# One weight split behind the first sums of x, one bank copy ahead of a cast, in the first pair of gate and up

## The chip, the core and the metric

The kernel runs on one core of a Trainium2 chip. The core's engines work side by side, each through its own list of instructions in order: TensorE (PE) multiplies matrices into eight banks of PSUM, VectorE (DVE) and ScalarE (ACT) do elementwise work, GpSimd (POOL) does a little of it, and SyncE (SP) issues the transfers from memory. They wait for each other through semaphores. The metric is the time of one execution on the device, in microseconds (us); smaller is better. The engine names of the profile are used below; L506 is line 506 of the kernel.

## What is computed

A decoder trunk of two layers over 512 positions of width 1024. Each layer is a mixer (convolution and attention in layer 0, linear and latent attention in layer 1), a layer norm, a dense SwiGLU feed-forward net of width 2816, and a layer norm. The change lies in the feed-forward net, which comes once in each layer:

```python
def swiglu(x, w_gate, w_up, w_down):
    return (jax.nn.silu(x @ w_gate) * (x @ w_up)) @ w_down

x = layer_norm(ALPHA * x + y, ln_mix_g[layer], ln_mix_b[layer])
x = layer_norm(ALPHA * x + swiglu(x, ffn_w_gate[layer], ffn_w_up[layer], ffn_w_down[layer]),
               ln_ffn_g[layer], ln_ffn_b[layer])
```

All inputs and outputs are float32.

## The kernel before

**Numbers in two parts.** Every float32 operand of a matrix product is split into a rounded high part and the rest: a cast on ACT writes the high part, a subtraction on DVE the low part (`split`, lines 97 to 104). A product is then three matmuls: high by high, high by low, low by high.

**Gate and up** (`ffn`, from line 379). x is held transposed in `xh` and `xl` (high and low part), eight tiles of 128 features by 512 positions. Its four blocks of 128 positions come out of the layer norm one after the other; `flip` transposes a block on PE (L275), casts it into `xh` on ACT (L279), subtracts into `xl` on DVE (L280), and then copies it to a float32 tile `m` on ACT (L284). The first two tiles of 128 gate and up columns are computed directly, as four weights with one bank each. `lower` multiplies the first 256 positions, and takes the last two blocks through their flips in between; `upper(0)` and `upper(1)` multiply the other 256 positions, for the first and the second of these tiles; `finish` takes the silu on ACT (L393) and multiplies on DVE (L394).

**The pairs.** The other 20 tiles are done in pairs, each by seven products in place of eight, after Winograd's form of Strassen's method (`sevens`, from line 443). It works on sums of quarters of the weights and sums of quarters of x:

- `sums(sx)` makes the sums of x once in each layer. `s1` is the first of them: two differences on DVE (L355), and their split into tiles `hx` (cast on ACT, subtraction on DVE). `s2_sum` and `s2` (L361, L366, L367), `s3` and `s4` (L372 and splits) follow.
- `total(i)` makes the sum of weights that product i needs, if it needs one: on DVE (L483), into the tiles `lng` and `lnb`, or by an accumulating transfer that POOL issues (L474, for i = 4).
- `make(i)` issues the fetches that are due (`fetch_for`, L459, on SP), calls `total` for i + 1, and splits weight i. For i = 5 the call of `total(6)` comes after the split.
- `take(i)` runs product i on PE (L506, 24 matmuls of 256 columns; the first pairs open a bank with one matmul of 512 columns, the prime of L521) and moves the result on. In this method a bank is passed on: `take(0)` copies its bank to a second one (L533), `take(1)` copies its bank to a tile (L537), `take(2)` copies its bank to a third one (L541) to which the product of `take(4)` then adds, and `take(4)` copies that to a fourth (L549) to which `take(6)` adds.

Weights are split up to four products ahead (AHEAD = 4). There are five buffers for fetched weights and five for split ones.

**The order** is written out by hand: inside `tc.manual_schedule` (line 398) the instructions of each engine run in the order in which the program makes them. So a call that is moved in `ffn` moves its instructions in the queues of PE, ACT, DVE, POOL and SP alike, and an instruction that waits holds up all that stand behind it on its engine. `down`, which multiplies by the third weight, follows the pairs, and the kernel goes through `mixer0`, `ffn`, `mixer1`, `ffn`.

Of the kernel before, what the change touches and what calls it, by code (L numbers as in the profile page):

```python
# [34 lines left out]
AHEAD = 4  # L35
# [10 lines left out]
def trunk(ctx, tc, a, out):  # L46
# [21 lines left out]
    def nm(s):  # L68
        cnt[0] += 1
        return f"{s}{cnt[0]}"  # L70

    def slot(dt=F32):
        return wk.tile([P, 512], dt, tag="wk", name=nm("wk"))
# [305 lines left out]
    def ffn(layer, last, flips):  # L379
        hs = []  # L380
        m8 = {}

        def hidden_tile(f):
            if f < WK:
                return slot()
            if not m8:
                m8["t"] = big.tile([P, 8, S], F32, tag="m8", name=nm("m8"))
            return m8["t"][:, f - WK, :]

        def finish(f, pg, pu):  # L390
            h = hidden_tile(f)
            t = temp()
            act(out=t, in_=pg, func=AF.Silu)  # L393
            tt(out=h, in0=t, in1=pu, op=ALU.mult)  # L394
            hs.append(h)

        E = mybir.EngineType
        with tc.manual_schedule(engines={E.PE, E.Activation, E.DVE, E.Pool, E.SP}):
            first, sx = [], {}

            def lower(flip):
                w, bank = first[-1]
                gemm_a(bank, w, cols=slice(0, 256), ks=range(4))
                if flip:
                    flips.pop(0)()
                gemm_a(bank, w, cols=slice(0, 256), ks=range(4, KD))

            def upper(f):
                for w, bank in first[2 * f:2 * f + 2]:
                    gemm_a(bank, w, cols=slice(256, 512))  # L410

            ready = state["ready"]
            for i in range(4):
                first.append((ready.pop(0), ps()))
                if i < 2:
                    ready.append(weight())
                if i == 3:
                    make, take, n = sevens(sx, hs, hidden_tile)
                    make(0)
                lower(i % 2)  # L420
            s1, s2_sum, s2, s3, s4 = sums(sx)
            s1()
            upper(0)
            finish(0, first[0][1], first[1][1])
            s2_sum()
            upper(1)
            make(1)
            make(2)
            finish(1, first[2][1], first[3][1])
            s2()  # L430
            make(3)
            take(0)
            s3()
            make(4)
            s4()
            for i in range(AHEAD + 1, n + AHEAD):
                if i < n:
                    make(i)
                take(i - AHEAD)
        gb = load_ln("ffn", layer)  # L440
        return down(hs, [1] * (KF - 5) + [5], gb, last)

    def sevens(sx, hs, hidden_tile):

        pairs = list(range(DIRECT, KF, 2))
        n = 7 * len(pairs)
        base = state["i"]  # L450
        state["i"] += 4 * len(pairs)
        state["sums"] = 0
        raw, ws, tiles = {}, {}, {}

        def fetch_quarter(p, name, which):

            raw[p, name] = rawp.tile([P, D], F32, tag="raw", name=nm("raw"))
            i = base + 4 * p + which
            nc.sync.dma_start(out=raw[p, name], in_=a["w"][i // 2, :, (i % 2) * D:(i % 2) * D + D])  # L459


        loads = {}
        for p in range(len(pairs)):
            for at, args in ((-5, ("x", 0)), (-4, ("u", 1)), (-2, ("y", 2)), (-1, ("z", 3))):
                loads.setdefault(7 * p + at, []).append((p, *args))

        def total(i):

            if i >= n:
                return  # L470
            p, pos = divmod(i, 7)
            if pos == 4 and p == 0:
                q = base + 2
                nc.gpsimd.dma_start(out=raw[p, 4], in_=a["w"][q // 2, :, (q % 2) * D:(q % 2) * D + D],  # L474
                                    accum_op=ALU.add)
            elif pos == 4:
                tt(out=raw[p, 4], in0=raw[p, "u"], in1=raw[p, "y"], op=ALU.add)
            elif pos in (1, 2, 6):
                tag = ("lng", "lnb")[state["sums"] % 2]
                state["sums"] += 1  # L480
                raw[p, pos] = big.tile([P, D], F32, tag=tag, name=nm(tag))
                r, s = {1: ("x", "u"), 2: (1, "y"), 6: (2, "z")}[pos]
                tt(out=raw[p, pos], in0=raw[p, r], in1=raw[p, s], op=ALU.add)  # L483

        def make(i):

            fetch_for(i)
            p, pos = divmod(i, 7)
            raw[p, 4] = raw[p, "u"]
            if i != 5:  # L490
                total(i + 1)
            hi, lo = pair()
            split(raw[p, ("x", 1, 2, "z", 4, "y", 6)[pos]], hi, lo)
            if i == 5:
                total(i + 1)
            ws[i] = [t.rearrange("p (f k m) -> p f k m", f=2, k=4) for t in (hi, lo)]

        def quarter(k0, t0):
            return [[t[:, k0 + 2 * j:k0 + 2 * j + 2, t0:t0 + 256] for j in range(2)] for t in (xh, xl)]

        def product(bank, w, x, start=True):
            hi, lo = w
            for f in range(2):
                for k in range(4):
                    for m, (l, r) in enumerate(((hi, x[0]), (hi, x[1]), (lo, x[0]))):
                        mm(bank[:, f * 256:f * 256 + 256], lhsT=l[:, f, k, :], rhs=r[k // 2][:, k % 2, :],  # L506
                           start=(start and f == 0 and k == 0 and m == 0), stop=(k == 3 and m == 2),
                           skip_group_check=True)

        def take(i):  # L510


            p, pos = divmod(i, 7)
            g = tiles
            w = ws.pop(i)

            def primed():

                bank = ps()
                if p == 0 or (p == 1 and pos == 0):  # L520
                    mm(bank, lhsT=w[0][:, 0, 0, :], rhs=xh[:, 0, :], start=True, stop=True)  # L521
                return bank

            def half(n, gate, up):
                for f in range(2):
                    c = slice(f * 256, f * 256 + 256)
                    stt(out=g["h"][f][:, n * 256:n * 256 + 256], in0=gate[:, c], scalar=-1.0, in1=up[:, c],
                        op0=ALU.mult, op1=ALU.mult)

            if pos == 0:  # L530
                g["a"], g["d"] = ps(), primed()
                product(g["a"], w, quarter(0, 0))
                nc.scalar.copy(out=g["d"], in_=g["a"])  # L533
            elif pos == 1:
                g["b"], g["p5"] = ps(), temp("p")
                product(g["b"], w, sx["s1"])
                nc.scalar.copy(out=g["p5"], in_=g["b"])  # L537
            elif pos == 2:
                g["e"] = primed()
                product(g["d"], w, sx["s2"], start=False)  # L540
                nc.scalar.copy(out=g["e"], in_=g["d"])  # L541
            elif pos == 3:
                product(g["a"], w, quarter(4, 0), start=False)
                g["g0"] = temp()
                act(out=g["g0"], in_=g["a"], func=AF.Silu)
            elif pos == 4:
                product(g["e"], w, sx["s3"], start=False)
                g["f"], g["up1"] = primed(), temp("p")
                nc.scalar.copy(out=g["f"], in_=g["e"])  # L549
                tt(out=g["up1"], in0=g["p5"], in1=g["e"], op=ALU.add)  # L550
            elif pos == 5:
                product(g["d"], w, sx["s4"], start=False)
                up0 = temp("p")
                tt(out=up0, in0=g["p5"], in1=g["d"], op=ALU.add)
                g["h"] = [hidden_tile(pairs[p] + f) for f in range(2)]
                half(0, g["g0"], up0)
            else:
                product(g["f"], w, quarter(4, 256), start=False)
                g1 = temp()
                act(out=g1, in_=g["f"], func=AF.Silu)  # L560
                half(1, g1, g["up1"])
                hs.extend(g["h"])

        def fetch_for(i):
            for args in loads.get(i, ()):
                fetch_quarter(*args)

        for at in range(-5, 0):
            fetch_for(at)
        return make, take, n  # L570


    def mixer0():
# [658 lines left out]
```

## Time and profile before

| | |
|---|---|
| runs without a profile | 1083.64, 1085.29, 1083.64 us; median 1083.64 |
| the profiled execution, its own time | 1085.82 us |
| its span, from the first to the last instruction | 1083.9 us |
| mean granted clock of TensorE in it | 0.994 of full speed |
| gate and up, layer 0: from the first lower half to the last product | about 173 to 406 us |
| gate and up, layer 1 | about 724 to 956 us |

The profile is one execution, recorded by the chip; times in it count from the first instruction. Its views are: busy time by engine; who waited for whom; the instructions of one engine in order of time (the timeline: start, duration, engine, line, operation, output and inputs, count; in brackets the idle time before it and who ended that); and stretches of time (windows), with the busy time of each engine and then the granted clock, the share of the transfer engines, and GB/s. In the timeline neighbours of one kind are merged; the duration of a merged row reaches from the first start to the last end, and the matmuls in it follow each other faster than one of them lasts, since they are pipelined. How far apart they start is read from the starts of two rows and the count between them.

### The profile page before, as it was taken

The page shows a single profiled execution, that of the slowest core. Times are in us where ns is not written, and L with a number is a line of the kernel's source. Part 1 is how long each engine was busy: PE and PEld are TensorE (multiplying, and loading weights), DVE is VectorE, ACT ScalarE, POOL GpSimd, SP SyncE. Part 2 cuts the span into 40 slices and gives each one's busy share as a digit, 9 for nine tenths or more (in the row PEclk, how much of TensorE's full clock was granted, in tenths as well). Part 3 has the DMA queues.
Part 4 walks back from the last instruction along what each step waited for, and adds up shares of the span by engine and source line. Part 5 has one row for each costly group of instructions (what it writes and reads, how often), then busy time and mean ns, then how long its engine had stood idle before and what let it go on. Part 6 is the DMA issues. An engine that isn't in the chain of part 4 may idle for free.

```text
span 1083.9 us, 16990 instructions
## 1 busy us (share of the span) xinstructions
PE 1067.7 (99%) x6936; PEld 964.4 (89%) x6936; DVE 726.5 (67%) x1122; ACT 498.1 (46%) x831; POOL 61.6 (6%) x98
## 2 busy tenths in 40 slices
PE   9999999999999999999999999999999999999997
PEld 7888888999999998888988888889999999988885
DVE  5666549887787773334857895488878778753337
ACT  4544335645545562223467454355555454542221
POOL 0000000000000000000513421000000000000001
PEclk9999999999999999999999999999999999999998
DMA  9522222333323343331342030322432322443302
GB/s 340 197 76 79 78 79 72 85 97 101 120 92 109 121 160 118 97 98 59 98 136 79 2 117 4 112 70 73 133 98 85 130 98 92 152 147 97 97 1 77
DMA packets 31789, 110.43 MB, mean 102 GB/s; under 512 B 3536, under 2 KB 3680, under 8 KB 31712
## 3 DMA queue, kind: packets, MB, share of 16 engines
q1 hardware_dynamic: 31424, 108.31, 30.7%
q0 software_dynamic: 288, 1.05, 0.5%
q8 instruction: 54, 0.88, 0.3%
q14 instruction: 23, 0.19, 0.1%
HBM read 107.25 MB, written 2.10 MB: 101 GB/s over the span
## 4 chain that ended last, share of the span: by engine, by line
PE 88%; DVE 7%; ACT 3%; issue 1%; DMA 0%; POOL 0%; DVEq 0%; SPq 0%; ACTq 0%; POOLq 0%
PE ps L506 35%; PE ps L297 27%; PE ps L179 11%; PE ps L213 6%; PE ps L958 1%; DVE w L104 1%; PE ps L883 1%; DVE xn L259 1%; ACT w L98 1%; DVE p L256 1%; DVE p L234 1%; PE ps L806 1%; PE ps L655 1%; PE ps L602 1%; ACT hx L98 1%
## 5 line engine op out<-in xcount | busy, mean ns | idle before, releaser
L297 PE MATMUL ps<-w,hx 128*128 128x512 f32 x1440 | 329.4, 390 | 0.0
L297 PEld LDWEIGHTS ps<-w,hx 128*128 128x128 f32 x1440 | 269.6, 188 | 55.5
L104 DVE TENSOR_TENSOR w<-raw,w 128x1024 fp32r<-128x1024 f32 (+1 forms) x181 | 219.7, 1219 | 67.4 <-ACT w L98 61.4
L506 PE MATMUL ps<-xh,w 128*128 128x256 f32 x1280 | 237.6, 283 | 0.0
L98 ACT CAST w<-raw 128x1024 fp32r<-128x1024 f32 (+2 forms) x184 | 189.5, 1038 | 61.0 <-PE ps L506 23.7
L506 PEld LDWEIGHTS ps<-xh,w 128*128 128x128 f32 x1280 | 200.8, 189 | 0.0
L506 PE MATMUL ps<-hx,w 128*128 128x256 f32 x1440 | 182.8, 286 | 4.4 <-ACT ps L541 4.4
L506 PEld LDWEIGHTS ps<-hx,w 128*128 128x128 f32 x1440 | 178.8, 192 | 4.9 <-ACT ps L541 4.8
L506 PE MATMUL ps<-xl,w 128*128 128x256 f32 x640 | 181.3, 283 | 0.0
L179 PE MATMUL ps<-xh,w 128*128 128x512 f32 (+1 forms) x608 | 162.1, 350 | 0.8 <-ACT xh L98 0.8
L179 PEld LDWEIGHTS ps<-xh,w 128*128 128x128 f32 x608 | 107.1, 191 | 16.4 <-ACT xh L98 1.5
L506 PEld LDWEIGHTS ps<-xl,w 128*128 128x128 f32 x640 | 120.9, 189 | 0.3
L179 PE MATMUL ps<-xl,w 128*128 128x512 f32 (+1 forms) x304 | 105.7, 348 | 1.3 <-DVE xl L280 1.3
L104 DVE TENSOR_TENSOR hx<-m,hx 128x512 fp32r<-128x512 f32 x32 | 21.6, 691 | 80.9 <-ACT hx L98 80.9
L179 PEld LDWEIGHTS ps<-xl,w 128*128 128x128 f32 x304 | 58.0, 191 | 8.7 <-DVE xl L280 1.7
L252 POOL TENSOR_TENSOR rs<-ve,neghalf 128x1 f32<-128x1 f32 x16 | 10.5, 656 | 881.4 <-DVE ve L250 838.3
L213 PE MATMUL ps<-w,xh 128*128 128x512 f32 (+1 forms) x192 | 58.2, 384 | 0.0
L98 ACT CAST hx<-m 128x512 fp32r<-128x512 f32 x32 | 19.3, 622 | 83.2 <-PE ps L297 83.1
L104 DVE TENSOR_TENSOR hx<-wk,hx 128x512 fp32r<-128x512 f32 x28 | 19.3, 691 | 51.8 <-ACT hx L98 51.7
L104 DVE TENSOR_TENSOR w<-lng,w 128x1024 fp32r<-128x1024 f32 x30 | 36.8, 1226 | 21.9 <-ACT w L98 21.9
L104 DVE TENSOR_TENSOR w<-lnb,w 128x1024 fp32r<-128x1024 f32 x30 | 36.8, 1225 | 20.8 <-ACT w L98 20.7
L98 ACT CAST hx<-wk 128x512 fp32r<-128x512 f32 x28 | 17.4, 621 | 64.0 <-PE ps L297 61.4
(217 smaller groups left out, 1099.5 us busy)
## 6 DMA issues: line engine op xcount, KB each, us to landing
raw<-in_w_dram SPq DMA_DIRECT2D x182, 512.0 KB, 4.0
hx<-in_xT_dram SPq DMA_DIRECT2D x8, 256.0 KB, 5.9
xn<-in_xn_dram SPq DMA_DIRECT2D x4, 512.0 KB, 9.4
out_dram<-xn SPq DMA_DIRECT2D x8, 256.0 KB, 2.0
raw<-in_w_dram SPq DMA_DIRECT2D x4, 256.0 KB, 5.9
lng<-in_ln_mix_g_dram SPq DMA_DIRECT2D x2, 512.0 KB, 7.4
lnb<-in_ln_mix_b_dram SPq DMA_DIRECT2D x2, 512.0 KB, 8.1
raw<-in_w_dram POOLq DMA_DIRECT2D x2, 512.0 KB, 7.3
```

The lines of the kernel that those rows point to most:

```text
L98: nc.scalar.copy(out=hi, in_=src)
L104: tt(out=lo, in0=src, in1=hi.bitcast(F32), op=ALU.subtract)
L179: mm(dst[:, cols], lhsT=l[:, k, :], rhs=r[:, k, cols], start=(k == 0 and n == 0), stop=(k == KD - 1 and n == 2))
L213: mm(banks[b][:, :n], lhsT=l[:, k, t], rhs=r[:, c], start=(k == 0 and m == 0), stop=(k == KD - 1 and m == 2))
L234: stt(out=r[h], in0=xn[:, b, h * 512:h * 512 + 512], scalar=ALPHA, in1=acc[h], op0=ALU.mult, op1=ALU.add)
L256: stt(out=r[h], in0=r[h], scalar=neg, in1=g[:, hs], op0=ALU.add, op1=ALU.mult)
L259: state["ln"] = stt(out=xn[:, b, hs], in0=r[h], scalar=rs, in1=be[:, hs], op0=ALU.mult, op1=ALU.add)
L297: mm(acc[b][h], lhsT=l[:, bs], rhs=r[:, h * 512:h * 512 + 512], start=(k == 0 and n == 0), stop=(k == nk - 1 and n == 2))
L506: mm(bank[:, f * 256:f * 256 + 256], lhsT=l[:, f, k, :], rhs=r[k // 2][:, k % 2, :], start=(start and f == 0 and k == 0 and m == 0), stop= ...
L602: mm(banks[s][bank][:, o:o + n], lhsT=l[rows[s], b * P:(b + 1) * P], rhs=r[rows[s], (b + 1) * P - n:(b + 1) * P], start=(i == 0), stop=(i ...
L655: mm(po[rows[s], b * P:(b + 1) * P], lhsT=vn[:, j * P + 64 * s:j * P + 64 * s + 64], rhs=loc[s][(b, half)], start=(half == 0 or b == 0), s ...
L806: mm(dst, lhsT=x[:, c], rhs=y, start=(k == 0 and n == 0), stop=(k == nk - 1 and n == 2))
```

## The change

Two calls are moved. The split of weight 0 (`make(0)`) goes from ahead of the last lower half to behind `s1()`; the sum for weight 1, which `make(0)` also made, stays where it was, as a call of `total(1)` of its own. And at the start of the pairs `take(2)`, with its bank copy, goes ahead of `make(6)`. The rest serves these two: `sevens` hands out `total`, and a name that `make` set is set in `total`.

```diff
@@ ffn
                 if i == 3:
-                    make, take, n = sevens(sx, hs, hidden_tile)
-                    make(0)
+                    total, make, take, n = sevens(sx, hs, hidden_tile)
+                    total(1)
                 lower(i % 2)
             s1, s2_sum, s2, s3, s4 = sums(sx)
             s1()
+            make(0)
             upper(0)
             finish(0, first[0][1], first[1][1])
             s2_sum()
@@ ffn
             s3()
             make(4)
             s4()
-            for i in range(AHEAD + 1, n + AHEAD):
+            make(5)
+            take(1)
+            take(2)
+            make(6)
+            for i in range(AHEAD + 3, n + AHEAD):
                 if i < n:
                     make(i)
                 take(i - AHEAD)
@@ sevens, total
             p, pos = divmod(i, 7)
+            raw[p, 4] = raw[p, "u"]
@@ sevens, make
             p, pos = divmod(i, 7)
-            raw[p, 4] = raw[p, "u"]
-            if i != 5:
+            if 0 < i != 5:
                 total(i + 1)
@@ sevens
-        return make, take, n
+        return total, make, take, n
```

Before, the order at this place was `make(5)`, `take(1)`, `make(6)`, `take(2)`, `make(7)`, `take(3)`; after, it is `make(5)`, `take(1)`, `take(2)`, `make(6)`, `make(7)`, `take(3)`. The layers share the code, so both are changed alike.

## The prediction

> **What bounds the kernel now.** I read the page first, then TensorE's waits, then its timeline at the two places that the waits name, then ScalarE and VectorE there.
>
> ```profile
> PE 1067.7 (99%) x6936; PEld 964.4 (89%) x6936; DVE 726.5 (67%) x1122; ACT 498.1 (46%) x831; POOL 61.6 (6%) x98
> ```
>
> TensorE (PE) is busy 99% of the span, so only time in which it stands still, or runs slowly, can be won without taking work away. The view of waits for PE lists the few places where it stands still; the columns are total us, times, longest.
>
> ```profile
> PE ps L506 <- ACT ps L541: 4.4, 2, 2.4
> PE ps L179 <- DVE xl L280: 1.3, 2, 0.7
> ```
>
> Both come twice, once in each layer's gate and up, and both are touched by the change. The timeline of PE in layer 0 (start us, duration us):
>
> ```profile
> 186.45 0.40 PE L179 MATMUL ps<-xh,w 128*128 128x256 f32 x2
> 187.51 0.39 PE L179 MATMUL ps<-xl,w 128*128 128x256 f32 x1 [0.66 <-DVE xl L280]
> ...
> 202.12 3.04 PE L506 MATMUL ps<-hx,w 128*128 128x256 f32 x24
> 205.00 0.40 PE L521 MATMUL ps<-xh,w 128*128 128x512 f32 x1
> ...
> 210.87 0.28 PE L506 MATMUL ps<-xh,w 128*128 128x256 f32 x1
> 213.54 4.63 PE L506 MATMUL ps<-hx,w 128*128 128x256 f32 x24 [2.39 <-ACT ps L541]
> 218.01 0.40 PE L521 MATMUL ps<-xh,w 128*128 128x512 f32 x1
> ```
>
> A product of 24 matmuls takes 205.00 - 202.12 = 2.88 us, 0.12 a matmul. Product 3 issues its last matmul at 210.87; product 4 could follow at 210.99 and starts at 213.54. It then takes 218.01 - 213.54 = 4.47 us for the same 24 matmuls. The same places in layer 1:
>
> ```profile
> 737.21 0.40 PE L179 MATMUL ps<-xh,w 128*128 128x256 f32 x2
> 738.27 0.39 PE L179 MATMUL ps<-xl,w 128*128 128x256 f32 x1 [0.66 <-DVE xl L280]
> ...
> 761.64 0.28 PE L506 MATMUL ps<-xh,w 128*128 128x256 f32 x1
> 763.96 4.63 PE L506 MATMUL ps<-hx,w 128*128 128x256 f32 x24 [2.04 <-ACT ps L541]
> 768.42 0.40 PE L521 MATMUL ps<-xh,w 128*128 128x512 f32 x1
> ```
>
> Why product 4 is slow stands in the view by windows. The granted clock is the third number from the end.
>
> ```profile
> 187.00:190.00 3.00, 2.48 (x20) 2.49 (x21) 2.35 (x4) 1.74 (x3) 0.37 (x1) 1.00 0.62 157
> 213.54:214.50 0.96, 0.96 (x7) 0.96 (x8) 0.96 (x2) 0.96 (x2) 0.00 (x0) 0.95 0.76 273
> 214.80:217.90 3.10, 3.10 (x17) 3.10 (x17) 3.10 (x4) 1.20 (x2) 0.00 (x0) 0.51 0.34 104
> 765.00:767.00 2.00, 2.00 (x11) 2.00 (x11) 2.00 (x3) 1.42 (x2) 0.00 (x0) 0.50 0.39 152
> ```
>
> After each long stall PE gets half its clock for some 3 us; after the short one it stays at 1.00.
>
> Who holds product 4? It adds to a bank that ScalarE (ACT) must first fill with the sums of product 2 (line 541). ACT and VectorE (DVE), in their order:
>
> ```profile
> 208.49 1.04 ACT L98 CAST w<-raw 128x1024 fp32r<-128x1024 f32 x1
> 209.44 0.58 ACT L537 COPY p<-ps 128x512 f32<-128x512 f32 x1
> 211.96 1.04 ACT L98 CAST w<-lng 128x1024 fp32r<-128x1024 f32 x1 [1.94 <-DVE lng L483]
> 212.91 0.58 ACT L541 COPY ps<-ps 128x512 f32<-128x512 f32 x1
> ```
>
> ```profile
> 209.56 1.23 DVE L104 TENSOR_TENSOR w<-raw,w 128x1024 fp32r<-128x1024 f32 x1 [0.26 <-ACT w L98]
> 210.71 1.22 DVE L483 TENSOR_TENSOR lng<-lnb,raw 128x1024 f32<-128x1024 f32 x1
> ```
>
> The cast of weight 6 waits 1.94 us for a sum on DVE, and the copy stands behind it, though the product that it copies issued its last matmul before 208.2 (205.00, a prime of double width, 0.24, and 24 x 0.12 make 208.1).
>
> **Part one: the copy ahead of cast 6.** ACT's order becomes cast 5, copy 537, copy 541, cast 6. By the row of copy 537 ACT is free for the next at about 209.95, so copy 541 would end at about 210.5 even if nothing else moved, ahead of 210.99. Removed: 213.54 - 210.99 = 2.55 us in layer 0 and 763.96 - 761.76 = 2.20 in layer 1. With the stall I expect the half clock to go: 4.47 - 2.88 = 1.59 and 768.42 - 763.96 - 2.88 = 1.58. The last two rest on one reading, that the stall draws the half clock; their bounds are nothing (no clock over 1.00 is granted) and 1.59.
>
> The wait is not gone but now stands in the copy, which waits for product 2, with casts 6 and 7 and a silu queued behind it on ACT. It costs nothing while product 2 ends ahead of the sum for cast 6 at 211.93; the margin is over 3 us. Cast 6 keeps its time, and so does everything DVE does after it. The only DMAs issued in the moved steps are make(6)'s on SP; the takes that they pass issue none, so the order on SP stays, and POOL's accumulating DMA belongs to make(3) as before.
>
> [...]
>
> **Part two: split 0 behind the first sums.** DVE and ACT around the first stall:
>
> ```profile
> 184.50 1.22 DVE L483 TENSOR_TENSOR lng<-raw,raw 128x1024 f32<-128x1024 f32 x1
> 185.64 1.22 DVE L104 TENSOR_TENSOR w<-raw,w 128x1024 fp32r<-128x1024 f32 x1
> 186.78 1.28 DVE L280 TENSOR_TENSOR xl<-ps,xh 128x512 fp32r<-128x512 f32 x2
> ...
> 193.51 0.69 DVE L394 TENSOR_TENSOR wk<-tmp,ps 128x512 f32<-128x512 f32 x1 [2.13 <-ACT w L98]
> ```
>
> ```profile
> 187.49 1.18 ACT L284 COPY m<-ps 128x512 f32<-128x512 f32 x2 [1.57 <-DVE xl L280]
> 189.44 1.22 ACT L98 CAST hx<-tmp 128x512 fp32r<-128x512 f32 x2 [0.76 <-DVE tmp L355]
> ...
> 192.47 1.04 ACT L98 CAST w<-lng 128x1024 fp32r<-128x1024 f32 x1
> ```
>
> The sub of split 0 (185.64) stands ahead of the two xl subs that PE waits for. Without it the first xl sub starts at 185.64 and its half is there at 186.3; PE wants it at 186.69 (two matmuls from 186.45, 0.12 each). So the matmul of 187.51 goes at 186.69: 0.82 us, and 738.27 - 737.45 = 0.82 in layer 1.
>
> The split is not saved, it is moved. The copies of line 284, the differences of x and the hx casts come 186.78 - 185.64 = 1.14 us earlier, so ACT ends the hx casts at about 189.5. Cast 0 (1.04 like cast 1) then runs to 190.55. Queued behind it on ACT are the table load and silu (the 1.81 us between 190.66 and 192.47) and cast 1, which come some 0.1 earlier than now. Sub 0 (1.22) runs on DVE from 190.55 to 191.8, with line 394 queued behind it; what hides it is the idle 2.13 us ahead of that line, and uncovered it would cost 1.22 a layer.
>
> Line 394 reads the silu's output and the second bank of the upper half. Of that half's 48 matmuls the second goes at 187.51, so the last goes 46 x 0.12 later, at some 193.1, and with the 0.28 of one such row ends at 193.4. It will end 0.82 earlier. But cast 1 ends at 193.51 as well, exactly where line 394 starts. If line 394 waits for it, it comes only 0.1 earlier, and the chain behind it is 0.7 later against PE than in the first case. Between these ends I take the first, since the line reads nothing of cast 1; the second is rival 2.
>
> Product 0 starts at 202.12 - 2.88 = 199.24 now and 0.82 earlier then, far behind 191.8, where weight 0 is ready. One fetch waits for sub 0, since it takes the buffer:
>
> ```profile
> 186.89 0.33 SPq L459 DMA_DIRECT2D raw<-in_w_dram  x1
> ```
>
> ```profile
> raw<-in_w_dram SPq DMA_DIRECT2D x182, 512.0 KB, 4.0
> ```
>
> ```profile
> 214.18 1.22 DVE L483 TENSOR_TENSOR lnb<-raw,raw 128x1024 f32<-128x1024 f32 x1
> ```
>
> It brings u of the second pair (line 464), is issued at about 191.8 instead, and lands some 4 us later, by the page's median for such transfers. The sum of line 483 at 214.18 is the first to read it, so this is free.
>
> **What is late next.** With both stalls gone product 4 starts at 210.99 - 0.82 = 210.17 in layer 0, product 5 (2.88 and a prime later) at 213.29, product 6 at 216.17. Product 6 needs the copy of line 549, which on ACT stands behind cast 8, and that behind the sum of 214.18, which ends at 215.40 now and 0.82 earlier then: cast 8 to 215.55, copy to 216.1. That is just in time. In layer 1 the stall was 0.35 shorter for the same work, so there the copy is some 0.3 us early. I take 0.05 off for it. What comes after has room: weight 7 is split behind the sum of 214.18, by about 216 then, and product 7 asks for it at 219.
>
> **The sum.** 0.82 + 0.82 + 2.55 + 2.20 + 1.59 + 1.58 - 0.05 = 9.5 us. Behind it PE runs without a gap, so the gain is kept. The profiled execution took 1085.82 us (span 1083.9), hence 1076.3. The runs' median is 1083.64, 2.18 less, hence 1074.1 if the same stalls are in it. The runs differ by 1.65 us (1083.64 and 1085.29), about the price of one slow stretch; if the median run lacks one, it has 1.6 less to win and ends at 1075.7. I take 1075.0, between these two; both belong to the forecast.
>
> **The rivals.**
> 1. The half clock stays: it comes from PE's load over a longer stretch and not from the stall. For it: in layer 0 it starts only about 1 us after PE has restarted (0.95 in 213.54:214.50). Against it: it shows at no other place of this stage. It keeps 3.17 us: a gain of 6.3, so 1077.3 from the median. [...]
> 2. The stall moves on: line 394 waits for cast 1, the chain is 0.7 later against PE. Copy 541 then ends at 210.4 (0.2 us of stall), and copy 549 costs product 6 some 0.5 more; in layer 1 about 0.3 in all. Too short to draw the half clock. Gain 8.5: 1075.1 to 1076.7.
> 3. The change doesn't do what it says: copy 541 is not what held product 4, but something beside it that comes at the same time. The copy ends at 212.91 + 0.58 = 213.49 and product 4 starts at 213.54, so little speaks for it. Only part two is left: 1.6 us, 1082.0, no change by measure.
> 4. Slower: the copy, now ahead of cast 6, holds ACT's queue while it waits for product 2. That costs from the point where product 2 ends after 211.93, 3.7 us later than now, and then a microsecond each; to lose over 0.2% it must hold some 6 us in each layer beyond that. PE would have to be late by some 9 us at product 2, which no row hints at. About 1086.
>
> **How the numbers follow.** Forecast 0.66, rival 1 0.12, rival 2 0.16, rival 3 0.03, rival 4 0.03. The forecast's own range is 1074.0 to 1076.4. The range 1073.5 to 1077.6 takes in rivals 1 and 2 and leaves the others out. About 0.2% (2.2 us) is what a measurement of this kernel tells from no change. Faster: the first three, 0.94; within: rival 3, 0.03; slower: rival 4, 0.03.
>
> **What would show it.** In PE's waits the lines L541 and L280 vanish; product 4 follows product 3 at 0.12 us and takes 2.9; the clock is 1.00 in the whole stage. A wait on the copy of line 549 ahead of product 6 would be rival 2, a clock of 0.5 without a stall rival 1, a stall of the old length ahead of product 4 rival 3, and casts 6 to 8 later than now rival 4. The forecast falls if the stall is gone and the span is not shorter by about 9.

## The result, and the profile after

| | before | after |
|---|---|---|
| median of the runs compared | 1084.42 us (4 runs, 1083.64 to 1085.29) | 1077.1 us (4 runs, 1075.94 to 1078.76) |
| ratio after to before, 95% interval | | 0.9933 [0.9914, 0.9953] |
| the profiled execution, its own time | 1085.82 | 1078.24 |
| its span | 1083.9 | 1076.3 |
| mean granted clock in it | 0.994 | 0.996 |

The change makes the kernel faster by 7.3 us, or 0.7%. The time is inside the stated range and 2.1 us above the stated time; it is also above the forecast's own range, 1074.0 to 1076.4.

PE's waits in the profile after (total us, times, longest):

```profile
PE ps L148 <- DVE hx L146: 1.4, 1, 1.4
PE ps L179 <- ACT xh L98: 0.9, 1, 0.9
PE ps L1015 <- ACT wk L1007: 0.2, 1, 0.2
```

Both waits that the change aimed at are gone; what is left lies at the start and in the second mixer. PE's timeline around product 4 of layer 0 (lines behind 418 are some lines further down in the changed kernel: L506 is L511, L521 is L526, L541 is L546, L549 is L554):

```profile
210.24 0.28 PE L511 MATMUL ps<-xh,w 128*128 128x256 f32 x1
210.36 3.04 PE L511 MATMUL ps<-hx,w 128*128 128x256 f32 x24
213.24 0.40 PE L526 MATMUL ps<-xh,w 128*128 128x512 f32 x1
213.47 3.04 PE L511 MATMUL ps<-hx,w 128*128 128x256 f32 x24
216.40 0.38 PE L511 MATMUL ps<-xh,w 128*128 128x256 f32 x1
```

Product 4 follows product 3 at 0.12 us and takes 213.24 - 210.36 = 2.88 us, against 4.47 before. The granted clock (third number from the end) is 1.00 over these stretches of both layers, where it was 0.91 before:

```profile
200.00:220.00 20.00, 20.00 (x165) 19.77 (x164) 18.20 (x22) 12.30 (x17) 0.00 (x0) 1.00 0.33 106
760.00:780.00 20.00, 20.00 (x168) 19.91 (x167) 19.54 (x21) 12.14 (x16) 0.00 (x0) 1.00 0.44 140
```

Product 6 comes at 216.40 where it could have come at 213.47 + 2.88 = 216.35. ACT there:

```profile
207.86 1.04 ACT L98 CAST w<-raw 128x1024 fp32r<-128x1024 f32 x1
208.81 0.58 ACT L542 COPY p<-ps 128x512 f32<-128x512 f32 x1
209.28 0.59 ACT L546 COPY ps<-ps 128x512 f32<-128x512 f32 x1
211.33 1.05 ACT L98 CAST w<-lng 128x1024 fp32r<-128x1024 f32 x1 [1.46 <-DVE lng L489]
...
214.80 1.06 ACT L98 CAST w<-lnb 128x1024 fp32r<-128x1024 f32 x1 [0.98 <-DVE lnb L489]
215.76 0.59 ACT L554 COPY ps<-ps 128x512 f32<-128x512 f32 x1
```

The copy of L546 is done at 209.87, half a microsecond ahead of product 4; cast 6 waits as before, now behind it. The copy of L554 ends at 216.35: this is the 0.05 us that product 6 waits. DVE around the split that was moved:

```profile
185.91 1.29 DVE L280 TENSOR_TENSOR xl<-ps,xh 128x512 fp32r<-128x512 f32 x2
...
190.79 1.23 DVE L104 TENSOR_TENSOR w<-raw,w 128x1024 fp32r<-128x1024 f32 x1 [0.26 <-ACT w L98]
192.88 0.69 DVE L394 TENSOR_TENSOR wk<-tmp,ps 128x512 f32<-128x512 f32 x1 [0.86 <-PE ps L179]
```

Sub 0 (190.79) lies in the idle time ahead of line 394, and 0.86 us of that idle time are left. Cast 1 on ACT runs past the start of line 394:

```profile
192.57 1.04 ACT L98 CAST w<-lng 128x1024 fp32r<-128x1024 f32 x1
```

**Where the time went.** The chain that ended last has a row for the first matmul of each `down` (L297): it starts with the mixer's and, behind gate and up, with that of the feed-forward net. The differences of these starts cut the span into stages. Before:

```profile
127.85 27.21 PE ps L297 x120
...
405.82 110.20 PE ps L297 x486
...
689.52 16.37 PE ps L297 x72
...
956.24 119.72 PE ps L297 x528
```

After:

```profile
128.11 35.37 PE ps L297 x156
...
401.21 110.19 PE ps L297 x486
...
686.61 24.52 PE ps L297 x108
...
948.63 119.72 PE ps L297 x528
```

| stage | before | after | difference |
|---|---|---|---|
| up to the first of these matmuls | 127.85 | 128.11 | +0.26 |
| with gate and up of layer 0 | 277.97 | 273.10 | -4.87 |
| down, and the second mixer | 283.70 | 285.40 | +1.70 |
| with gate and up of layer 1 | 266.72 | 262.02 | -4.70 |
| the last down to the end | 127.66 | 127.67 | 0.0 |
| span | 1083.9 | 1076.3 | -7.6 |

The stages that the change touches win 9.57 us. But the second mixer, which it doesn't touch, loses 1.70. The clock there (third number from the end), and PE's timeline:

```profile
640.00:642.00 2.00, 1.76 (x12) 1.44 (x12) 1.21 (x3) 1.18 (x3) 0.00 (x0) 0.89 0.67 197
642.00:644.00 2.00, 2.00 (x6) 1.55 (x6) 1.16 (x4) 0.20 (x1) 0.00 (x0) 0.50 0.33 131
644.00:646.00 2.00, 2.00 (x9) 1.67 (x8) 1.64 (x5) 0.00 (x0) 0.00 (x0) 0.75 0.04 8
```

```profile
638.45 1.95 PE L984 MATMUL ps<-pack,tmp 128*128 128x2 f32 x16
640.26 0.85 PE L1006 MATMUL ps<-pack,tmp 128*128 128x128 f32 x6
641.35 4.54 PE L1015 MATMUL ps<-wk,wk 128*128 128x256 f32 x12 [0.24 <-ACT wk L1007]
```

Before, the same matmuls stood on line 1010:

```profile
645.95 2.86 PE L1010 MATMUL ps<-wk,wk 128*128 128x256 f32 x12 [0.24 <-ACT wk L1002]
```

The 12 matmuls took 2.86 us before and take 4.54 now. PE's clock is halved here for some 3 us (0.50 in 642:644; it was 1.00 in 644:646 and 646:648 before), without a stall of note (0.24 us): what stands ahead of it are 16 matmuls of two columns each, 1.9 us in which PE counts as busy and computes almost nothing, and six transposes.

### The profile page after: what moved, and what is told of

The parts are those of the page before. It is cut to its first block, busy times and chain, and to the rows that moved or that the text cites. A ratio compares the mean times of both kernels' runs of the same rounds, so it can differ in the third digit from the quotient of the medians.

```text
span 1076.3 us, 16992 instructions
## 1 busy us (share of the span) xinstructions
PE 1065.7 (99%) x6936; PEld 962.4 (89%) x6936; DVE 725.6 (67%) x1122; ACT 499.2 (46%) x831; POOL 61.6 (6%) x98
## 4 chain that ended last, share of the span: by engine, by line
PE 99%; DMA 0%; DVE 0%; ACT 0%; issue 0%; DVEq 0%; SPq 0%
PE ps L511 37%; PE ps L297 30%; PE ps L179 16%; PE ps L213 6%; PE ps L963 1%; PE ps L275 1%; PE ps L888 1%; PE ps L811 1%; PE ps L660 1%; PE ps L607 1%; PE ps L647 1%; PE ps L861 0%; PE ps L877 0%; PE ps L1015 0%; DMA hx<-in_xT_dram 0%; PE ps L859 0%
## 5 line engine op out<-in xcount | busy, mean ns | idle before, releaser
L297 PE MATMUL ps<-w,hx 128*128 128x512 f32 x1440 | 329.4, 390 | 0.0
L297 PEld LDWEIGHTS ps<-w,hx 128*128 128x128 f32 x1440 | 269.5, 188 | 55.6
L511 PE MATMUL ps<-xh,w 128*128 128x256 f32 x1280 | 237.7, 283 | 0.0
L511 PEld LDWEIGHTS ps<-xh,w 128*128 128x128 f32 x1280 | 201.7, 190 | 0.1
L511 PE MATMUL ps<-xl,w 128*128 128x256 f32 x640 | 181.2, 283 | 0.0
L511 PE MATMUL ps<-hx,w 128*128 128x256 f32 x1440 | 179.6, 283 | 0.0
L511 PEld LDWEIGHTS ps<-hx,w 128*128 128x128 f32 x1440 | 175.9, 190 | 0.1
L511 PEld LDWEIGHTS ps<-xl,w 128*128 128x128 f32 x640 | 121.8, 190 | 0.3
```

What stands on the lines that cost most here:

```text
L297: mm(acc[b][h], lhsT=l[:, bs], rhs=r[:, h * 512:h * 512 + 512], start=(k == 0 and n == 0), stop=(k == nk - 1 and n == 2))
```

## The experiments

Four questions: do the two parts add up (e1, e2), does the stall draw the half clock (e3, e5, b2, b3), what is the slow stretch in the mixer (a2, e4, e6, e7, a3), and can it be taken away. Times of one table row are those of all its runs; the last columns count the runs by their mean clock. One half-clock stretch of 1.7 us costs about 0.0016 of the mean clock (1.7 of 1076), so the columns are about none, one, and two or more stretches. This is an estimate: the mean clock does not say where a stretch lies (e5's profile has 0.996 by a stretch at 8 to 12 us, with 0.82 in 5:10 and 0.84 in 10:15), e2's profile has 0.995 with two of them, and of the last column one run of before, 1084.90 us with a clock of 0.945, fits no count.

| kernel | runs | shortest | median | 0.997 up | 0.995, 0.996 | 0.994 down |
|---|---|---|---|---|---|---|
| before, beside the experiments | 51 | 1083.33 | 1084.75 | 0 | 28 | 23 |
| after, with a2 and a3 | 16 | 1075.68 | 1077.24 | 6 | 10 | 0 |
| e1, copy only | 6 | 1077.36 | 1078.01 | 5 | 1 | 0 |
| e2, split only | 11 | 1080.56 | 1083.52 | 1 | 9 | 1 |
| e3, stall filled | 11 | 1082.51 | 1083.66 | 4 | 7 | 0 |
| e5, stall half filled | 11 | 1082.47 | 1083.70 | 3 | 8 | 0 |
| e4 and e7, dense mixer | 11 | 1075.61 | 1076.52 | 11 | 0 | 0 |
| e6, thin work doubled | 5 | 1079.73 | 1081.08 | 0 | 5 | 0 |

### e1: the copy alone

```diff
-            for i in range(AHEAD + 1, n + AHEAD):
+            make(5)
+            take(1)
+            take(2)
+            make(6)
+            for i in range(AHEAD + 3, n + AHEAD):
```

> The kernel before with part one alone: take(2) and its bank copy ahead of make(6). Theory (the copy frees product 4, and the stall drew the half clock): PE's waits for L541 vanish in both layers, product 4 takes 2.88 us at a clock of 1.00, the two waits for xl (L280, 0.66 each) stay. 7.9 us less than the kernel before where neither has a slow stretch elsewhere: some 1077.6 in the shortest runs. Rival 1 (the half clock is not the stall's doing): product 4 still takes about 4.4 us, gain 4.8, some 1079 to 1081.

Ratio 0.9942 [0.9927, 0.9958]; the shortest runs 1077.36 and 1077.52. In its profile the wait for L541 is gone and this one stays:

```profile
PE ps L179 <- DVE xl L280: 1.3, 2, 0.7
```

By the same starts of L297 as above, the stage of layer 0 took 403.50 - 129.53 = 273.97 us and that of layer 1 952.16 - 689.23 = 262.93: gains of 4.00 and 3.79, where 4.14 and 3.78 were expected. Its profile has the slow stretch in the mixer too (0.83 in 640:650, L1014 in 4.54 us), so that stretch doesn't need the moved split.

### e2: the split alone

```diff
-                    make, take, n = sevens(sx, hs, hidden_tile)
-                    make(0)
+                    total, make, take, n = sevens(sx, hs, hidden_tile)
+                    total(1)
                 lower(i % 2)
             s1, s2_sum, s2, s3, s4 = sums(sx)
             s1()
+            make(0)
```

The lines in `sevens` that serve it are changed as in the whole change.

> The kernel before with part two alone: split 0 behind the first sums of x. Theory: the two waits for xl (L280) vanish, 0.82 us each; the waits for L541 stay at about 2.5 and 2.2 us with the half clock behind them, since PE and the chain both come 0.82 earlier. Gain 1.6, some 1082 to 1084. Rival 2 (line 394 waits for cast 1, so the chain does not follow PE): the waits for L541 grow by 0.7 each and the gain is about nothing.

Ratio 0.9986 [0.9975, 0.9996]. The stages took 404.14 - 127.07 = 277.07 and 953.70 - 687.90 = 265.80 us: 0.90 and 0.92 less than before. PE's long stalls stay to the hundredth:

```profile
211.84 4.64 PE L507 MATMUL ps<-hx,w 128*128 128x256 f32 x24 [2.39 <-ACT ps L542]
...
761.41 4.63 PE L507 MATMUL ps<-hx,w 128*128 128x256 f32 x24 [2.04 <-ACT ps L542]
```

So the chain on ACT and DVE came earlier by as much as PE, as the theory has it and rival 2 has not. With e1 the gains of layer 0 add up to 4.90 and those of layer 1 to 4.71, against 4.87 and 4.70 for the whole change: the parts are independent. One of the 11 runs took 1080.56 us with a clock of 0.998, some 3 us less than the rest: by its clock neither stall drew the half clock there, though no profile shows that run.

### e3 and e5: the stall filled with work

```diff
                 elif pos == 4:
+                g["f"] = ps()
+                if p == 0:
+                    for _ in range(9):
+                        mm(g["f"], lhsT=w[0][:, 0, 0, :], rhs=xh[:, 0, :], start=True, stop=True)
                 product(g["e"], w, sx["s3"], start=False)
-                g["f"], g["up1"] = primed(), temp("p")
+                if p == 0:
+                    mm(g["f"], lhsT=w[0][:, 0, 0, :], rhs=xh[:, 0, :], start=True, stop=True)
+                g["up1"] = temp("p")
```

e5 has 4 in the place of 9. The bank is overwritten by its prime afterwards.

> The kernel before, with nine matmuls of 512 columns added ahead of product 4 of the first pair, into a bank that is overwritten afterwards: 9 x 0.235 = 2.1 us of work in the place of the stall, the wait for the copy itself unchanged. Theory (idle PE draws the half clock): about 0.4 and 0.1 us of idle time are left, product 4 takes 2.88 us, the clock is 1.00 there, and the profiled span is 3.2 us shorter than that of the kernel before with both stretches, though work was added. Rival 1: product 4 still takes about 4.4 us at a clock of 0.5, and the time is that of before.

> The same with four matmuls in place of nine: 0.9 us of work, some 1.6 and 1.3 us of idle time left ahead of product 4. Theory: the half clock needs a stall longer than the 0.82 us that drew none; whether 1.3 to 1.6 draw it is open. Drawn in both layers: the time of before. Drawn in none: 3.2 us less. Drawn in one layer or in some runs alone: it hangs on where the stall lies, not on its length alone.

PE in layer 0 of e3, then in e5 for both layers:

```profile
210.38 2.23 PE L550 MATMUL ps<-xh,w 128*128 128x512 f32 x9
212.94 3.13 PE L506 MATMUL ps<-hx,w 128*128 128x256 f32 x24 [0.33 <-ACT ps L541]
```

```profile
211.55 1.09 PE L550 MATMUL ps<-xh,w 128*128 128x512 f32 x4
214.10 3.13 PE L506 MATMUL ps<-hx,w 128*128 128x256 f32 x24 [1.46 <-ACT ps L541]
...
762.99 3.13 PE L506 MATMUL ps<-hx,w 128*128 128x256 f32 x24 [1.10 <-ACT ps L541]
```

The wait for the copy ends where it did, but product 4 takes 3.13 us by these rows, against 4.63 before, at a clock of 1.00 (e3's second stall, in layer 1, is gone altogether). Useless work makes the stage faster: by 1.47 us in layer 0 for e3 (403.74 - 127.24 = 276.50) and by 1.49 in layer 1 (954.36 - 689.13 = 265.23). So here it was idle PE that drew the half clock: 2.39 and 2.04 us of it did in the first profile (0.51 in 214.8:217.9, 0.50 in 765:767), and 1.46 and 1.10 us did not in e5's (1.00 in 213:217 and 762:766). That refutes rival 1 of the prediction for these stalls. Nor does chance explain it: the nine profiles in which the long stall is gone or filled show no half clock in gate and up of either layer (1.00 in every stretch of 10 us), and the four that have it show one behind seven of their eight stalls (0.83 in the 10 us around each of the seven, 1.00 around the eighth). The whole kernel won less than that: ratio 0.9987 [0.9977, 0.9997] for e3, 0.9993 [0.9984, 1.0002] for e5. In e3's profile the span is 1.9 us shorter, not 3.2: a slow stretch came at 644 to 647 in the mixer (0.83 in 640:650) in place of the two, and 7 of its 11 runs have a clock of 0.996; e5's profile has none there, and a lower clock in the first 20 us.

### b2 and b3: two more profiles of the kernel before

> The kernel before, unaltered, for a second profile. Theory: both waits for L541 as in the first profile (2.4 and 2.0 us); whether the half clock follows them in this execution too is open: the runs of before lie in groups at about 1083.8, 1085 and 1086.6, which says that the slow stretches do not come in all of them.

> The kernel before once more, for a third profile. The same: waits of 2.4 and 2.0 us for L541; a product 4 of 4.4 us or of 2.9 us, in each layer for itself.

b2 took 1084.26 us, b3 1086.4. Product 4 in b2, layer 0 and layer 1:

```profile
213.14 4.63 PE L506 MATMUL ps<-hx,w 128*128 128x256 f32 x24 [2.39 <-ACT ps L541]
...
763.89 3.14 PE L506 MATMUL ps<-hx,w 128*128 128x256 f32 x24 [2.04 <-ACT ps L541]
```

b3 has 4.58 and 4.62 us, as the first profile has 4.63 in both. The same stall of 2.04 us drew the half clock in two executions (0.50 in 765:767 of the first profile, 0.61 in 764:768 of b3) and not in a third (1.00 in 764:768 of b2). So the kernel before has executions with one stretch and executions with two. By the stage of layer 1 the difference is 1.48 us: 954.70 - 689.46 = 265.24 in b2 against 266.72 in the first profile and in b3.

### a2 and a3: the changed kernel again

> The changed kernel once more, unaltered, for more of its runs. Theory: both stalls of gate and up are gone in every run, no half clock there; the spread that is left (1075.94 to 1078.76 so far) comes from the first 25 us, where the clock is taken up, and from a slow stretch of 1.7 us in the second mixer (641 to 645 in the first profile), which comes in some executions only. So two or three groups of times from 1075.9 to about 1079, and a clock of 0.998 in the short ones, 0.996 in the long ones. Rival (the slow stretches are only moved from gate and up into the mixer, in every run): nearly all runs near 1078.

> The changed kernel unaltered, beside the two others on the same chip. Theory: about half of its runs have the slow stretch in the mixer (clock 0.996), the others not (0.998); 1075.8 to 1078.8.

Ratios 0.9928 [0.9913, 0.9943] and 0.9933 [0.9918, 0.9947]. Both profiles are of executions without the slow stretch in the mixer (1.00 in 640:644 of a2 and in 640:645 of a3; spans 1074.7 and 1073.8); in a2 L1015 reads

```profile
641.43 2.86 PE L1015 MATMUL ps<-wk,wk 128*128 128x256 f32 x12 [0.24 <-ACT wk L1007]
```

with the same stall of 0.24 as in the first profile, where it took 4.54. Of all 16 runs 10 have a clock of 0.995 or 0.996 and 6 have 0.998. Where the stretch of the ten lies is known for one of them, the first profile; the runs of e4 and e7 below say that it is mostly the mixer.

### e4 and e7: dense work between the thin matmuls and the transposes

```diff
         diagonal()
+        pg[0]()
         end_flip(0)
         end_flip(1)
         for c in range(3):
             state(c)
-        pg[0]()
         outputs(0)
```

> The changed kernel, with the first output gate's matmuls of the second mixer (24 of 512 columns, dense) put between the matmuls of two columns (line 984) and the transposes behind them. Theory (long stretches of matmuls that hardly load PE draw the half clock as idle time does): no slow stretch at 640 to 650, all runs at a clock of 0.998, the long group of times of the changed kernel is gone, shortest runs at 1075.9 or a few tenths less. Rival: the slow stretch comes from elsewhere (a fixed rhythm of the clock), it stays or moves, and the times spread as those of the changed kernel.

> The changed kernel with the dense matmuls of the output gate between the thin ones and the transposes, once more, for more of its runs. Theory: no run with the slow stretch of the mixer, clock 0.997 or above in all; about 0.5 to 1.0 us less than the changed kernel in the mean. Rival: the five runs without it were luck, and some of these have a clock of 0.996.

Ratios to before 0.9921 [0.9907, 0.9934] and 0.9922 [0.991, 0.9935], against 0.9928 and 0.9933 for the changed kernel in the same sets. The intervals overlap, but the clocks do not: no run of 11 is below 0.997, and 10 of 16 are without this edit. The means are 1076.51 and 1077.29 us. In e4's profile L1015 runs at full speed (1.00 in 640:650) behind a longer stall:

```profile
645.80 0.82 PE L1006 MATMUL ps<-pack,tmp 128*128 128x128 f32 x6
647.02 2.86 PE L1015 MATMUL ps<-wk,wk 128*128 128x256 f32 x12 [0.40 <-ACT wk L1007]
```

This kernel has the lowest mean of those that ran. The shortest runs are the same as without it (1075.61 and 1075.68): it takes away the long ones.

### e6: the thin matmuls doubled

```diff
-                for c in range(NB):
+                for c in (*range(NB), *range(NB)):
                     mm(pd[:, c * 4 + 2 * j:c * 4 + 2 * j + 2], lhsT=t[:, c * P:(c + 1) * P], rhs=sel,
                        start=True, stop=True)
```

> The changed kernel, with the 16 matmuls of two columns of the second mixer's diagonal (line 984) made twice, the second time over the first: 1.9 us more of work that hardly loads PE, nothing else altered. Theory (thin matmuls draw the half clock as idle time does, if enough of them fall together): the slow stretch of 1.7 us comes in every run, or nearly, instead of in six of ten; shortest runs at 1075.8 + 1.9 + 1.7 = 1079.4, clock 0.996 or below in all. Rival (the stretch comes by a rhythm that has nothing to do with this work): it comes as often as before, and the shortest runs are at 1077.7 with 0.998.

All five runs have a clock of 0.995 or 0.996, and the shortest took 1079.73 us, where 1079.4 was expected. PE's timeline and the clock:

```profile
637.73 4.74 PE L984 MATMUL ps<-pack,tmp 128*128 128x2 f32 x32
642.33 1.52 PE L1006 MATMUL ps<-pack,tmp 128*128 128x128 f32 x6
643.78 4.36 PE L1015 MATMUL ps<-wk,wk 128*128 128x256 f32 x12
```

```profile
640.00:642.00 2.00, 2.00 (x12) 2.00 (x11) 0.00 (x0) 0.00 (x0) 0.00 (x0) 0.50 0.68 211
642.00:644.00 2.00, 2.00 (x10) 1.67 (x10) 0.77 (x2) 0.59 (x2) 0.00 (x0) 0.50 0.11 43
644.00:646.00 2.00, 2.00 (x5) 1.57 (x6) 0.69 (x3) 0.88 (x2) 0.00 (x0) 0.50 0.03 8
646.00:648.00 2.00, 2.00 (x9) 1.65 (x8) 1.62 (x6) 0.00 (x0) 0.00 (x0) 0.79 0.00 0
```

The clock is halved from 640 on, while the thin matmuls still run and PE counts as busy all the time. It stays at 0.50 until 646.8, twice as long as in the first profile after the change (641.6 to 645.0). So the edit cost more here than the 1.9 + 1.7 = 3.6 us that were expected: `down` and the second mixer took 688.86 - 400.15 = 288.71 us, 5.0 more than in a3 (684.11 - 400.40 = 283.71), and that the shortest run came out near 1079.4 is in part luck.

With e4 and e7 this speaks for work that hardly loads PE as the cause of the mixer's stretch, and against a rhythm that has nothing to do with the work. In e6 the thin matmuls alone had brought the clock down before the first transpose. For the 16 of the changed kernel, the share of the six transposes and of the 0.24 us of idle time was not told apart.

## Why the prediction came out as it did

**The number** was in part lucky. The median, 1077.1 and 1077.24 over 16 runs, lies above the forecast's own range and in the stated one only because that was widened for rivals 1 and 2, neither of which came. The prediction also says that the forecast falls if the stall is gone and the span is not shorter by about 9 us. The span of the first profile is shorter by 7.6, so as a whole it did not come true in that execution; in those of a2 and a3 the span is shorter by 9.2 and 10.1.

**Part one** was right in mechanism and size: expected 2.55 + 1.59 and 2.20 + 1.58, measured alone 4.00 and 3.79. Of the 1.58 put down to the half clock in layer 1 some 1.48 is the clock: in b2 product 4 takes 2.98 us behind the same stall at full clock (from 763.89 to the next product's first matmul at 766.87), and not 2.88. The sum is the same, since both go with the stall.

**Part two** likewise: expected 0.82 a layer, measured 0.90 and 0.92. Line 394 starts at 192.88 while cast 1 runs until 193.61, so it never waited for it, and the choice between the two ends was the right one. Rival 2 falls.

**What is late next**: 0.05 us was taken off for product 6, and 0.05 is what it waits.

**The half clock**: rival 1 falls for the two stalls by e3, which kept the wait and lost the slow product. The sign named for it, a clock of 0.5 without a stall, did show, but in the second mixer (0.50 in 642:644, behind 0.24 us of idle time). Stalls of 2.39 us drew it in four profiles of four (three of before, e2), stalls of 2.04 in three of four, and 1.46 and 1.10 in none of one each. Why the stall of 2.04 draws nothing in b2 was not shown.

**The base** was open in the prediction: either the median run had both slow stretches, or it lacked one. b2 shows that it lacks one at times. By the clocks no run of before is without any, 28 have about one, and the other 23 mostly two, hence an estimate of about 1.5 in the mean.

**The step that failed** is "Behind it PE runs without a gap, so the gain is kept". PE does run without a new gap. But in the first profile 1.7 us are lost again to a half-clock stretch in the second mixer, which none of the three profiles of before shows there, and by their clocks 10 of 16 runs of the changed kernel have one such stretch. With e4 and e7, which alter only that mixer, none of 11 has. The prediction took stalls as the only cause of a half clock; work that hardly loads PE, which the busy time hides, went with one as well: in e6 the clock is 0.50 in 640:642, with PE busy for all of these 2.00 us. Put into the sum: 1075.7, the end of the forecast in which the median run lacks a stretch, and 1.7 x 10/16 = 1.1 make 1076.8, against 1077.1 in the first comparison and 1077.24 over 16 runs. The means tell the same: 1085.03 for 51 runs of before less 1077.29 for 16 of after is 7.7; the stalls alone are 2 x 0.92 + 2.55 + 2.20 = 6.6, and 1.5 - 0.6 slow stretches of some 1.6 us are an estimated 1.4 more, which makes 8.0.

**What stays open**: how often the mixer's stretch comes in the kernel before. Its runs can't be told apart by the mean clock, since the stretches of gate and up count alike. In the profiles it came in none of the four that had a slow product 4 in layer 0 (before, b2, b3, e2) and in three of the six that had none and left the mixer as it is (after, a2, a3, e1, e3, e5). That may be chance, or taking away one stretch makes the next one likelier; it wasn't tried further.

## What to carry to other kernels

On an engine that is busy 99% of the span, look for the few instructions behind which it stands, and ask what stands ahead of them in the queue of the engine that is waited for: a copy that is ready belongs ahead of a cast that still waits, and work with slack belongs behind work that somebody waits for. A stall of PE of two microseconds can cost more than its length: the stalls that stood for 2.55 and 2.20 us in the sum were worth 4.00 and 3.79 here, with a clock of 0.51 and 0.50 behind them. Suspect a run of matmuls of a few columns as if it were idle time, and put dense matmuls behind it; one place of this kernel shows that (with them no run of 11 has a clock below 0.997, without them 10 of 16 have). Before a gain of a few microseconds is summed up, see how far apart the runs of the same kernel lie, and by which steps.

## What the runs showed of the hardware that was not expected

- 16 matmuls of two columns (1.95 us) and six transposes, with PE busy throughout but for 0.24 us, are followed by some 3 us at half clock in some executions (0.50 in 642:644 of the first profile after the change, 1.00 in a2); 32 of them (4.74 us) bring the clock to 0.50 while they still run, and it stays there for 6.8 us. With 24 matmuls of 512 columns behind the 16, no mean clock of 11 runs shows such a stretch (0.997 to 0.999).
- Nine matmuls that compute nothing of use, put into a stall, made the stage of layer 0 faster by 1.47 us.
- The start of the kernel differs by up to 2.5 us between executions: the first matmul of the first `down` comes between 127.07 (e2) and 129.53 us (e1), with the same instructions ahead of it. The difference arises in the first 13 us, where PE ran at half its pace in e1 until 12.8 us, and in e2 at full pace from 7.3 us on at the latest. The granted clock reads 1.00 in both from 0 to 25 us, so this does not enter the mean clock; of the profiles only e5's has a lower one there (0.82 in 5:10, 0.84 in 10:15). One row of each, e1 first:

```profile
10.20 1.05 PE L179 MATMUL ps<-xh,w 128*128 128x512 f32 x2
```

```profile
9.70 0.63 PE L179 MATMUL ps<-xh,w 128*128 128x512 f32 x2
```
